# A second copy of x, laid out as features by tokens, in place of the transposes of x on TensorE

## The chip, the core and the metric

The kernel runs on one core of one Trainium2 chip. The metric is the device time of one execution in microseconds (us); lower is better. A core has five engines with a queue of instructions each: TensorE (PE; its weight loads are listed as PEld), VectorE (DVE), ScalarE (ACT), GpSimd (POOL) and SyncE (SP), which here issues nearly all DMA transfers. An engine works through its queue in order and waits on semaphores of the others. SBUF is the working memory of 128 partitions, PSUM the memory into which TensorE writes, in banks of 128 x 512 float32.

## The reference

Of the trunk in the reference only one layer is run (DEPTH is 1): sliding-window attention with a learned sink for each head, and a final norm.

```python
xn = rms_norm(x, norm_g)                       # x: 1 x 4096 x 1024, float32
q, k, v, z = split(xn @ w_in)                  # widths 1024, 256, 256, 1024
o = banded_attention(q, k, v, t5_table, 128, sinks)   # 16 heads of 64, 4 key groups, window 128
x = x + (merge_heads(o) * silu(z)) @ w_out     # w_out: 1024 x 1024
out = rms_norm(x, final_g)
```

rms_norm multiplies a token's row by 1 / sqrt(mean of its squares + 1e-6), the token's factor, and by a vector over the features.

## The kernel before

The 4096 tokens are worked on in 16 blocks of 256 (blocks 0 to 15 here, `tb` in the code, each of two halves `t` of 128 tokens). A product of float32 matrices is made of three products of float16 halves: each factor is split into a high half (rounded to float16, by ScalarE) and a low half (the rest, by VectorE), and high x high, high x low and low x high are summed in PSUM. The weights are loaded once, scaled and split (`load_w`, `split_w`), and the output weights are combined for Strassen's seven products, split and put back into DRAM (`split_wo`), from which each block loads them again (`load_s`).

What a block does with x. `load_x` brings two tiles `xin` of 128 tokens x 1024 features. `x_norm` sums the squares on ScalarE, into a tile `junk` that nobody reads, and gets the factors `rr` by VectorE and GpSimd. `x_scale` multiplies the tile by them, on ScalarE (in block 0 on VectorE); the factor is one number for each partition there, since tokens lie on the partitions. The projections need features on the partitions, so `x_turn` transposes 128x128 squares on TensorE into a PSUM bank `tp`, four for each of four calls, and splits the bank into the halves `xT`. The projections (`proj_t`, `proj_v`) go into banks `pj`; ScalarE and VectorE read them out to `q`, `k`, `v` and `z`. Attention is done by `Pair` objects, four for each block: scores into banks `s` (`scores`), bias and maximum on VectorE (`post`), exponentials on ScalarE (`exps`), sums, scaling and float16 halves `ph` (`halves`), their transposes into `tp` (`turn`), products with v into `o` (`values`) and the gate (`gate`). Then come seven output products (`split_y`, `product`, `add_product`), the residual `res` (loaded by `load_r`), the last norm (`out_norm`) and the store. A buffer is a slot in a rotating pool: the tag "ld" has 5 tiles of 512 KB for `xin`, `res` and the pieces of weights, "tp" has two PSUM banks, "op" four tiles for the halves of the output products.

The order of the work: the text lists every step in a table of slots, 28 for each block, and the steps of a block reach into the next block's slots (a block's x is prepared in the slots of the block before). The builder (`TileContext` with a simulated timeline) may then move an instruction ahead of others on its engine when its inputs are there earlier, so the order on an engine is that of the built program, not of the text. The lines in the text for x are

```python
at(before, s0 + (10 if tb else 4), load_x, tb + 1, t)
at(before, s0 + (12 if tb else 9), x_norm, tb + 1, t)
at(before, s0 + (14 if tb else 10), x_scale, tb + 1, t)
...
at(before, s0 + (18, 19, 25, 27)[j], x_turn, tb + 1, j)
```

Of the kernel before, what the change touches and what calls it, by code (L numbers as in the profile page):

```python
# [18 lines left out]
H = 16  # L19
# [12 lines left out]
# Powers of two that keep both halves of every split inside float16's normal range.  # L32
# [11 lines left out]
def one_hot_buckets():  # L44
    """Row b marks the places y of the circulant row where the distance (127 - y) mod 128 falls in bucket b."""
# [13 lines left out]
def tile_swa_block(ctx, tc, x, t5, norm_g, final_g, w_in, sinks, w_out, hot, out):  # L59
# [12 lines left out]
    # ---------------------------------------------------------------- loads that start at once  # L72
    gs = const.tile([P, KC], F32, name="gs")
    junk = const.tile([P, D], F16, name="junk")
    mhalf = const.tile([P, 1], F32, name="mhalf")
    nc.vector.memset(mhalf, -0.5)
    # The table of functions is loaded while the first inputs are on their way.
    nc.scalar.activation(junk[:, 0:1], mhalf, AF.Square)
    xin = {}

    def load_x(tb, t):
        xin[tb, t] = work.tile([P, D], F32, tag="ld", name="xin", bufs=5)
        r0 = tb * TB + t * P
        nc.sync.dma_start(xin[tb, t], x[r0:r0 + P, :])

# [8 lines left out]
    def load_w(n, j):  # L94
        tag, bufs = (("ld", 5), ("ws", 4))[j % 2]
        st = work.tile([P, 2, 512], F32, tag=tag, name="wst", bufs=bufs)
        src = w_in[2 * j * P:(2 * j + 2) * P, GROUPS[n]:GROUPS[n] + 512]
        nc.sync.dma_start(st, src.rearrange("(c p) f -> p c f", p=P))
        return st

    def split_w(n, j, st):
        for a in range(2):
            kc = 2 * j + a
            g1 = gs[:, kc:kc + 1]
            if n[0] == "z":
                # Heads (2 gp, r) and (2 gp + 1, r) share a block of 128 rows of the output.
# [11 lines left out]
    # Strassen's seven products for blocks of tokens by halves of the features: each one's factors, as signed blocks  # L118
    # (row, column), and the signed blocks of the result to which it goes.
# [11 lines left out]
    def combine(blocks, of):  # L131
        """The signed sum of one or two blocks."""
# [8 lines left out]
    def load_wo(c):  # L141
        st = []
        for gp in range(2):
            w = work.tile([P, D], F32, tag="ld", name="wst", bufs=5)
# [13 lines left out]
    # ---------------------------------------------------------------- constants  # L158
# [15 lines left out]
    # Masks the keys before the sequence's start, for the first block of queries alone.  # L174
# [7 lines left out]
    # ---------------------------------------------------------------- stages of a token block  # L182
    xs = {}

    def x_norm(tb, t):
        rs = work.tile([P, 1], F32, tag="rs", name="rs", bufs=2)
        nc.scalar.activation(junk, xin[tb, t], AF.Square, accum_out=rs)
# [6 lines left out]
    def x_scale(tb, t):  # L194
        if tb:
            nc.scalar.activation(xin[tb, t], xin[tb, t], AF.Copy, scale=xs[tb, t])
        else:
            nc.vector.tensor_scalar(xin[tb, t], xin[tb, t], xs[tb, t], None, op0=OP.mult)
# [3 lines left out]
    def x_turn(tb, j):  # L202
        """Two of the eight blocks of 128 features, transposed and split."""
        p = ps("tp", 2)
        pv = p.rearrange("p (c t) -> p c t", c=2)
        for a in range(2):
            for t in range(2):
                kc = 2 * j + a
                nc.tensor.transpose(pv[:, a, t * P:(t + 1) * P], xin[tb, t][:, kc * P:(kc + 1) * P], ident)
        d = work.tile([P, 2, 2, TB], F16, tag="xT", name="xT", bufs=6)  # L210
        nc.scalar.activation(d[:, :, 0, :], pv, AF.Copy)
        nc.vector.tensor_tensor(d[:, :, 1, :], pv, d[:, :, 0, :], op=OP.subtract)  # L212
# [10 lines left out]
    def proj_t(tb, n, c, p, a):  # L223
        """Features by tokens: block c of the weights n, into half a of a bank."""
# [9 lines left out]
    def evac_q(tb, gp, b, p):  # L234
        """Bank b of half gp: heads 4 b to 4 b + 3 of the half; float16 halves one above the other."""
# [44 lines left out]
    def evac_z(tb, gp, b, p):  # L280
        """2 PROJ silu(z) = (tanh(z / 2) + 1) PROJ z"""
# [345 lines left out]
```

## Time and profile before

| | |
|---|---|
| median of 3 runs | 1498.71 us (1497.95 to 1503.4) |
| the profiled execution: span from its first to its last instruction | 1502.1 us |
| TensorE busy | 1444.3 us, 96%, 12086 matmuls |
| VectorE busy | 1160.7 us, 77%, 3410 instructions |
| ScalarE busy | 740.7 us, 49%, 2036 instructions |
| GpSimd busy | 276.0 us, 18%, 251 instructions |
| DMA | 194.21 MB, 129 GB/s on average |

The profile page gives no time for its execution beside the span; the span is inside the range of the three runs. Busy time is the time in which an engine has at least one instruction under way. TensorE's matmuls are pipelined: the next begins while the last one's end is on its way, so the listed durations add up to more than the time that they take, and the time between the starts of neighbours says what one costs in a full queue.

### The profile page before, as it was taken

What the parts mean: (1) busy time and instruction counts of PE and PEld (TensorE: products, weight loads), DVE (VectorE), ACT (ScalarE), POOL (GpSimd) and SP (SyncE); (2) the same over time, 40 slices, a digit from 0 to 9 for tenths busy, and PEclk for the clock granted to TensorE, in tenths of its full rate; (3) what the DMA queues carried; (4) which work ended last, traced back from release to release, by engine and by line L of the source; (5) the groups of instructions that cost most, each with busy time, mean ns of one, the idle gap of its engine ahead of it and who ended that gap; (6) DMA issues with size and microseconds to landing.
All of it is one profiled execution on the core that took longest, in us unless ns stands there. A gap on an engine that the chain in (4) does not pass through costs nothing. (4 is left out here: it accounts for less than half of the span.)

```text
span 1502.1 us, 31168 instructions
## 1 busy us (share of the span) xinstructions
PE 1444.3 (96%) x12086; PEld 1089.4 (73%) x12086; DVE 1160.7 (77%) x3410; ACT 740.7 (49%) x2036; POOL 276.0 (18%) x251
## 2 busy tenths in 40 slices
PE   7869999999999999999999999999999999999996
PEld 6757777777768777777777777777777776777862
DVE  8799777778777777777778777787777777777896
ACT  8555454535545445454535545445454444544453
POOL 0241212102121211212102121111212112121123
PEclk9989999999999999999999999999999999999998
DMA  9764343514244242343413234241342523334065
GB/s 305 214 218 130 114 138 113 170 61 141 81 133 149 85 155 76 108 141 113 163 64 129 97 114 168 84 149 59 132 141 91 166 80 104 124 113 155 8 217 168
DMA packets 60501, 194.21 MB, mean 129 GB/s; under 512 B 7456, under 2 KB 9536, under 8 KB 60352
## 3 DMA queue, kind: packets, MB, share of 16 engines
q1 hardware_dynamic: 59312, 192.22, 39.1%
q8 instruction: 94, 1.54, 0.4%
q14 instruction: 55, 0.45, 0.1%
q10 hardware_dynamic: 1040, 0.00, 0.0%
HBM read 167.03 MB, written 25.17 MB: 128 GB/s over the span
## 5 line engine op out<-in xcount | busy, mean ns | idle before, releaser
L228 PE MATMUL pj<-xT,wh_q 128*128 128x256 f16 x2048 | 357.2, 275 | 0.8 <-DVE xT L212 0.5
L228 PE MATMUL pj<-xT,wh_z 128*128 128x256 f16 x2048 | 348.9, 273 | 0.1
L373 ACT ACTIVATE c<-c,nm 128x128 f32<-128x128 f32 x512 | 199.0, 389 | 254.0 <-DVE nm L367 254.0
L456 PE MATMUL pj<-ws,yo 128*128 128x512 f16 x1344 | 313.8, 381 | 2.5 <-DMA ws<-wos 1.6
L228 PE MATMUL pj<-xT,wl_q 128*128 128x256 f16 x1024 | 281.0, 275 | 0.0
L228 PE MATMUL pj<-xT,wl_z 128*128 128x256 f16 x1024 | 279.9, 273 | 0.0
L456 PEld LDWEIGHTS <-yo 128*128 128x128 f16 x1344 | 127.9, 98 | 142.6 <-issue 11.4
L228 PEld LDWEIGHTS <-wh_q 128*128 128x128 f16 x2048 | 199.3, 99 | 33.2 <-issue 11.3
L228 PEld LDWEIGHTS <-wh_z 128*128 128x128 f16 x2048 | 196.7, 98 | 36.5 <-issue 12.8
L470 POOL TENSOR_TENSOR res<-res,mc 128x512 f32<-128x512 f32 x80 | 102.3, 1278 | 516.6 <-ACT mc L465 383.9
L138 POOL TENSOR_TENSOR sum<-y 128x512 f32<-128x512 f32 x80 | 106.7, 1342 | 456.8 <-DVE y L427 284.5
L349 DVE COPY_PREDICATED s<-sel,s 128x128 f32<-128x128 int32 x256 | 72.7, 289 | 110.7 <-PE s L339 108.7
L387 ACT ACTIVATE ph<-c 128x512 f16<-128x512 f32 x128 | 80.2, 626 | 105.1 <-DVE c L385 100.8
L339 PE MATMUL s<-k,q 128*128 128x192 f16 x1024 | 126.6, 247 | 4.3 <-DVE c L356 4.2
L358 DVE CUSTOM_DVE_ANT_0 c<-s,bias 128x128 f32<-128x128 f32 x496 | 122.6, 284 | 2.8
L398 PE MATMUL tp<-ident,ph 128*128 128x128 f16 x1024 | 92.4, 221 | 29.6 <-ACT ph L387 19.3
L242 ACT ACTIVATE q<-pj 64x512 f16<-64x512 f32 x128 | 75.4, 589 | 83.8 <-PE pj L228 81.2
L401 DVE TENSOR_TENSOR po<-tp,own_m 128x1024 f16<-128x1024 f16 x128 | 87.9, 686 | 34.9 <-PE tp L398 34.3
L398 PEld LDWEIGHTS <-ph 128*128 128x128 f16 x1024 | 68.2, 98 | 62.3 <-ACT ph L387 32.9
L228 PEld LDWEIGHTS <-wl_z 128*128 128x128 f16 x1024 | 100.4, 98 | 17.1 <-issue 5.8
L228 PEld LDWEIGHTS <-wl_q 128*128 128x128 f16 x1024 | 100.9, 99 | 12.3 <-issue 0.5
L381 DVE TENSOR_TENSOR ls<-l,es 128x4 f32<-128x4 f32 x128 | 60.2, 471 | 62.8 <-ACT es L376 61.1
(89 smaller groups left out, 2358.4 us busy)
## 6 DMA issues: line engine op xcount, KB each, us to landing
ws<-wos SPq DMA_DIRECT2D x224, 512.0 KB, 4.7
xin<-in_x SPq DMA_DIRECT2D x32, 512.0 KB, 6.2
res<-in_x SPq DMA_DIRECT2D x32, 512.0 KB, 5.1
out<-res SPq DMA_DIRECT2D x32, 512.0 KB, 5.7
wst<-in_a_w_in SPq DMA_DIRECT2D x20, 512.0 KB, 9.2
wos<-wo SPq DMA_DIRECT2D x28, 256.0 KB, 2.8
wst<-in_a_w_out SPq DMA_DIRECT2D x16, 256.0 KB, 4.0
scr<-row SPq DMA_DIRECT2D x1, 1024.0 KB, 15.8
```

The costliest lines, as they stand in the source:

```text
L138: nc.gpsimd.tensor_tensor(s, of(a, b), of(c, d), op=OP.add if sign > 0 else OP.subtract)
L228: nc.tensor.matmul(p[:, a * TB:(a + 1) * TB], wx(n, wi, kc, c), xx(tb, xi, kc), start=k == 0, stop=k == 23)
L242: nc.scalar.activation(dst, pv[e * HD:(e + 1) * HD], AF.Copy, scale=SQ / PROJ)
L339: nc.tensor.matmul(s[:, hp, 0:3 * HD], lhs, rhs, start=hl == 0, stop=hl == 1)
L349: nc.vector.copy_predicated(dst, sel[:, None, :].to_broadcast([P, 2, HD]), src)
L358: nc.vector.tensor_tensor_reduce(out=cu, in0=sv, in1=b, scale=1.0, scalar=-3e38, op0=OP.add, op1=OP.max, accum_out=self.m[e][:, u:u + 1])
L373: nc.scalar.activation(cu, cu, AF.Exp, bias=nm[:, u:u + 1], scale=1.0 / SCORE, accum_out=self.l[e][:, u:u + 1])
L387: nc.scalar.activation(ph[:, 0], c, AF.Copy, scale=SP)
L398: nc.tensor.transpose(p[:, l, 2 * hp:2 * hp + 2, r * HD:(r + 1) * HD], self.ph[e][:, l, u, :], ident16)
L401: nc.vector.tensor_tensor(self.po[e], p8, own_m[:, None, :].to_broadcast([P, 8, P]), op=OP.mult)
L456: nc.tensor.matmul(p, YO[i][:, yi, c * P:(c + 1) * P], WO[i, c // 2][:, c % 2, wi, :], start=k == 0, stop=k == 11)
L470: nc.gpsimd.tensor_tensor(r, r, m, op=OP.add if sign > 0 else OP.subtract)
```

## The change

The host gives x a second time, `in_xt`: for each block of 256 tokens 128 partitions x 8 blocks of features x 256 tokens. `load_x` brings, besides `xin`, four tiles `xf` of 2 x 128 features by 256 tokens (256 KB each). `xin` is now used for the sums of squares alone. `x_row` turns the factors of the tokens into rows: a column of 128 factors, read as a 128x128 square with equal columns, is transposed on TensorE into a `tp` bank, twice for a block, so that every partition holds the 256 factors. `x_scale` multiplies an `xf` tile by this row in place, on VectorE, four times for a block. `x_split` makes the halves `xT` from `xf`, with the same two instructions as before, whose input lies in SBUF now.

To make room, "ld" has 4 tiles instead of 5, `junk` is a tile of the tag "op" instead of one of its own, and two small tiles of the bias's preparation share other tags. The products, the attention and the output are as before. Line numbers grow: 228 becomes 236, 398 becomes 406, 456 becomes 464.

```diff
     def load_x(tb, t):
-        xin[tb, t] = work.tile([P, D], F32, tag="ld", name="xin", bufs=5)
+        xin[tb, t] = work.tile([P, D], F32, tag="ld", name="xin", bufs=4)
         r0 = tb * TB + t * P
         nc.sync.dma_start(xin[tb, t], x[r0:r0 + P, :])
+        for j in (2 * t, 2 * t + 1):
+            xf[tb, j] = work.tile([P, 2, TB], F32, tag="xf", name="xf", bufs=4)
+            nc.sync.dma_start(xf[tb, j], xt[tb, :, 2 * j:2 * j + 2, :])
...
+    def junk():
+        return work.tile([P, D], F16, tag="op", name="junk", bufs=4)
...
-        nc.scalar.activation(junk, xin[tb, t], AF.Square, accum_out=rs)
+        nc.scalar.activation(junk(), xin[tb, t], AF.Square, accum_out=rs)
...
-    def x_scale(tb, t):
-        if tb:
-            nc.scalar.activation(xin[tb, t], xin[tb, t], AF.Copy, scale=xs[tb, t])
-        else:
-            nc.vector.tensor_scalar(xin[tb, t], xin[tb, t], xs[tb, t], None, op0=OP.mult)
+    rows = {}
+
+    def x_row(tb):
+
+        p = ps("tp", 2)[:, 0:TB]
+        for t in range(2):
+            nc.tensor.transpose(p[:, t * P:(t + 1) * P], xs[tb, t].to_broadcast([P, P]), ident)
+        rows[tb] = p
+
+    def x_scale(tb, j):
+        f = xf[tb, j]
+        nc.vector.tensor_tensor(f, f, rows[tb][:, None, :].to_broadcast([P, 2, TB]), op=OP.mult)
...
-    def x_turn(tb, j):
-        """Two of the eight blocks of 128 features, transposed and split."""
-        p = ps("tp", 2)
-        pv = p.rearrange("p (c t) -> p c t", c=2)
-        for a in range(2):
-            for t in range(2):
-                kc = 2 * j + a
-                nc.tensor.transpose(pv[:, a, t * P:(t + 1) * P], xin[tb, t][:, kc * P:(kc + 1) * P], ident)
+    def x_split(tb, j):
+
         d = work.tile([P, 2, 2, TB], F16, tag="xT", name="xT", bufs=6)
-        nc.scalar.activation(d[:, :, 0, :], pv, AF.Copy)
-        nc.vector.tensor_tensor(d[:, :, 1, :], pv, d[:, :, 0, :], op=OP.subtract)
+        nc.scalar.activation(d[:, :, 0, :], xf[tb, j], AF.Copy)
+        nc.vector.tensor_tensor(d[:, :, 1, :], xf[tb, j], d[:, :, 0, :], op=OP.subtract)
         xT[tb, j] = d
...
-                at(before, s0 + (14 if tb else 10), x_scale, tb + 1, t)
+            at(before, s0 + 16, x_row, tb + 1)
             for j in range(4):
-                at(before, s0 + (18, 19, 25, 27)[j], x_turn, tb + 1, j)
+                at(before, s0 + 17, x_scale, tb + 1, j)
+                at(before, s0 + (18, 19, 25, 27)[j], x_split, tb + 1, j)
...
+    x_row(0)
+    for j in range(4):
+        x_scale(0, j)
```

What this does to the order on the engines, at three places. On TensorE, in the middle of block 4's slots, before: behind the scores (`s`) of a pair come four transposes of x, then a projection (`pj<-xT`); such a group of four stands four times in a block.

```order
L339 LDWEIGHTS q
L339 MATMUL s<-k,q 128x192
L209 MATMUL tp<-ident,xin 128x128 x4
L228 LDWEIGHTS wh_q_79
L228 MATMUL pj<-xT,wh_q_79 128x256
```

And now, a little earlier in the same block: behind the products with v (`o<-pp,v`) stand the two transposes of the factors, then an output product (`pj<-ws,yo`).

```order
L426 LDWEIGHTS v
L426 MATMUL o<-pp,v 64x512
L207 MATMUL tp<-ident,rr 128x128 x2
L464 LDWEIGHTS yo
L464 MATMUL pj<-ws,yo 128x512
```

The four groups are gone from their places and one group of two stands ahead of the output product. The first transposes of the pair's softmax weights (L406) now stand 43 matmuls behind the second group of scores (31 of projections, 12 of an output product), where before (L398) they stood four transposes of x and 24 matmuls behind it.

On VectorE, at the same place of block 4, before: the sum of the exponentials and the scaling of the softmax weights (`ls`, `rl`, `c<-c,rl`), halves of output factors (`yo`), the low half of the softmax weights (`ph`) and the first low half of x (`xT<-tp`).

```order
L381 TENSOR_TENSOR ls<-l,es 128x4
L383 RECIPROCAL rl<-ls 128x4
L466 SCALAR_TENSOR_TENSOR res<-pj,res 128x512
L385 TENSOR_TENSOR c<-c,rl 128x512
L450 TENSOR_TENSOR yo<-sum,yo 128x512 x2
L450 TENSOR_TENSOR yo<-y,yo 128x512
L349 COPY_PREDICATED s<-sel,s 128x2x64
L388 SCALAR_TENSOR_TENSOR ph<-c,ph 128x512
L212 TENSOR_TENSOR xT<-tp,xT 128x2x256
```

And now: the four multiplications (`xf<-xf,tp`) stand ahead of that sum, and two low halves of x (`xT<-xf`) between it and the scaling.

```order
L212 TENSOR_TENSOR xf<-xf,tp 128x512 x4
L357 COPY_PREDICATED s<-sel,s 128x2x64
L389 TENSOR_TENSOR ls<-l,es 128x4
L220 TENSOR_TENSOR xT<-xf,xT 128x2x256
L366 ISA c,m<-s,bias 128x128
L366 ISA m 128x1
L366 ISA c,m<-s,bias 128x128
L366 ISA m 128x1
L391 RECIPROCAL rl<-ls 128x4
L474 SCALAR_TENSOR_TENSOR res<-pj,res 128x512
L458 TENSOR_TENSOR yo<-sum,yo 128x512
L220 TENSOR_TENSOR xT<-xf,xT 128x2x256
```

The sum, the scaling and the halves of this pair have moved behind the four multiplications and two splits.

In SP's queue at the start, before (`wst` are pieces of weights, `scr` and `bias` the table of biases): the bias is issued ahead of the last piece of the input weights.

```order
L98 DMA wst<-in_a_w_in 128x2x512 x5
L84 DMA xin<-in_x 128x1024 x2
L98 DMA wst<-in_a_w_in 128x2x512 x2
L305 DMA scr<-row 1024x1x256
L98 DMA wst<-in_a_w_in 128x2x512 x5
L310 DMA bias<-scr 64x8x192 x2
L98 DMA wst<-in_a_w_in 128x2x512
L147 DMA wst<-in_a_w_out 64x1024 x6
```

And now:

```order
L88 DMA xf<-in_xt 128x512 x3
L102 DMA wst<-in_a_w_in 128x2x512
L88 DMA xf<-in_xt 128x512
L102 DMA wst<-in_a_w_in 128x2x512 x2
L85 DMA xin<-in_x 128x1024
L102 DMA wst<-in_a_w_in 128x2x512 x2
L85 DMA xin<-in_x 128x1024
L102 DMA wst<-in_a_w_in 128x2x512
L313 DMA scr<-row 1024x1x256
L102 DMA wst<-in_a_w_in 128x2x512 x5
L318 DMA bias<-scr 64x8x192 x2
L151 DMA wst<-in_a_w_out 64x1024 x8
```

The transposed x of block 1 has come between the weights (that of block 0 stands ahead of all of them), and the bias has moved behind the last piece.

## Rows read from the trace of the kernel before

**Rows 1.** The page: busy time of each engine with its share of the span and its number of instructions, then the busy share of TensorE and VectorE in 40 equal slices, in tenths.

```profile
PE 1444.3 (96%) x12086; PEld 1089.4 (73%) x12086; DVE 1160.7 (77%) x3410; ACT 740.7 (49%) x2036; POOL 276.0 (18%) x251
PE   7869999999999999999999999999999999999996
DVE  8799777778777777777778777787777777777896
```

**Rows 2.** Busy time in three stretches: start and end, length, then for PE, PEld, DVE, ACT and POOL the busy time and the number of instructions, the granted clock of TensorE (1.00 is 2.4 GHz), the share of the DMA engines and GB/s.

```profile
155.00:1400.00 1245.00, 1228.77 (x10400) 932.21 (x10400) 945.26 (x2840) 601.19 (x1694) 212.19 (x192) 1.00 0.35 117
0.00:155.00 155.00, 126.91 (x1047) 102.17 (x1048) 131.85 (x342) 95.69 (x208) 36.29 (x36) 0.94 0.71 216
1400.00:1502.00 102.00, 88.61 (x644) 54.98 (x640) 83.54 (x229) 43.80 (x136) 27.56 (x23) 0.96 0.44 145
```

**Rows 3.** All waits of TensorE's matmuls in the stretch from 155 to 1400 us: who waited for whom, us in total, times, the longest.

```profile
PE tp L398 <- ACT ph L387: 11.3, 16, 1.3
PE tp L398 <- DVE ph L388: 2.6, 8, 0.5
```

**Rows 4.** Groups of TensorE's instructions in the same stretch: the transposes of x, their count, busy time and mean ns of one.

```profile
L209 PE MATMUL tp<-ident,xin 128*128 128x128 f32 x224 | 33.6, 273 | 0.0
```

**Rows 5.** Timeline of TensorE around a group of four transposes: start, time until the last one's end, line, tiles, count.

```profile
521.55 0.49 PE L339 MATMUL s<-k,q 128*128 128x192 f16 x4
...
521.88 0.60 PE L209 MATMUL tp<-ident,xin 128*128 128x128 f32 x4
...
522.32 0.38 PE L228 MATMUL pj<-xT,wh_q 128*128 128x256 f16 x2
```

**Rows 6.** Groups of the whole span by shape, for VectorE and ScalarE: busy time and mean ns of one, then the idle time ahead of them and what ended it.

```profile
L385 DVE TENSOR_TENSOR c<-c,rl 128x512 f32<-128x512 f32 x128 | 96.9, 757 | 2.5
...
L387 ACT ACTIVATE ph<-c 128x512 f16<-128x512 f32 x128 | 80.2, 626 | 105.1 <-DVE c L385 100.8 <-DVE mx L365 3.2
L466 DVE SCALAR_TENSOR_TENSOR res<-pj,res 128x512 f32<-128x512 f32 x112 | 75.9, 679 | 6.1 <-ACT mc L465 5.0
...
L450 DVE TENSOR_TENSOR yo<-sum,yo 128x512 f16<-128x512 f32 x80 | 54.8, 698 | 2.1 <-ACT yo L449 2.1
...
L212 DVE TENSOR_TENSOR xT<-tp,xT 128x512 f16<-128x512 f32 x64 | 43.5, 681 | 0.4 <-ACT xT L211 0.4
...
L211 ACT ACTIVATE xT<-tp 128x512 f16<-128x512 f32 x64 | 37.6, 588 | 4.5 <-PE tp L209 4.2
L450 DVE TENSOR_TENSOR yo<-y,yo 128x512 f16<-128x512 f32 x32 | 35.7, 1117 | 0.0
L196 ACT ACTIVATE xin<-xin,rr 128x1024 f32<-128x1024 f32 x30 | 34.0, 1135 | 0.0
```

**Rows 7.** The time around 525 us, in block 5's slots: the busy times from 519.65 to 532.57 us (columns as in rows 2), then pieces of the timelines of VectorE and GpSimd.

```profile
519.65:532.57 12.92, 12.92 (x114) 10.62 (x113) 12.64 (x33) 8.24 (x23) 5.40 (x4) 1.00 0.43 142
...
523.80 1.75 DVE L450 TENSOR_TENSOR yo<-y,yo 128x512 f16<-128x512 f32 x1
...
534.48 0.69 DVE L286 SCALAR_TENSOR_TENSOR z<-z,pj 128x512 f32<-128x512 f32 x1
535.09 0.68 DVE L401 TENSOR_TENSOR po<-tp,own_m 128x1024 f16<-128x1024 f16 x1
535.69 0.68 DVE L404 TENSOR_TENSOR pp<-tp,prev_m 128x1024 f16<-128x1024 f16 x1
...
523.36 1.65 POOL L138 TENSOR_TENSOR sum<-y 128x512 f32<-128x512 f32 x1 [1.23 <-DVE yo L450]
```

**Rows 8.** Timeline of TensorE: the first transposes of x for block 3 and for block 15.

```profile
250.60 0.60 PE L209 MATMUL tp<-ident,xin 128*128 128x128 f32 x4
...
1338.74 0.60 PE L209 MATMUL tp<-ident,xin 128*128 128x128 f32 x4
```

**Rows 9.** A row of all waits of the span: ScalarE's sum of squares waits for the load of x (columns as in rows 3).

```profile
ACT junk L187 <- DMA xin<-in_x: 90.0, 28, 7.4
```

**Rows 10.** Busy times in stretches of the first 100 us (columns as in rows 2).

```profile
0.00:20.00 20.00, 9.90 (x49) 7.38 (x50) 13.83 (x36) 15.34 (x26) 1.85 (x9) 1.00 0.94 326
20.00:40.00 20.00, 20.00 (x182) 17.37 (x180) 17.54 (x39) 16.51 (x26) 1.47 (x2) 1.00 0.98 292
...
60.00:80.00 20.00, 16.64 (x140) 13.74 (x138) 19.78 (x52) 12.05 (x35) 8.49 (x7) 0.92 0.56 175
80.00:100.00 20.00, 15.02 (x119) 11.65 (x116) 19.77 (x49) 10.02 (x24) 10.03 (x7) 0.83 0.67 212
...
60.00:65.00 5.00, 4.84 (x31) 3.53 (x30) 4.95 (x14) 3.02 (x6) 2.65 (x3) 0.68 0.67 217
...
80.00:85.00 5.00, 2.27 (x15) 1.61 (x13) 4.93 (x18) 2.88 (x6) 1.26 (x1) 0.53 0.55 179
```

**Rows 11.** The end of the weights' loading: from the timelines the issue of the last piece on SP's queue and who gets going with it on ScalarE, VectorE and TensorE (in brackets the idle time ahead of it and what ended it), and from the list of DMA issues the two transfers of the bias, KB each and median us to landing.

```profile
42.85 0.38 SPq L98 DMA_DIRECT2D wst<-in_a_w_in  x1
...
55.28 1.33 ACT L110 ACTIVATE wh_z<-wst,gs 128x512 f16<-128x512 f32 x2 [5.28 <-DMA wst<-in_a_w_in]
...
56.03 1.67 DVE L112 SCALAR_TENSOR_TENSOR wl_z<-wst,gs,wh_z 128x256 f16<-128x256 f32 x4 [4.97 <-ACT wh_z L110]
...
59.09 0.50 PE L339 MATMUL s<-k,q 128*128 128x192 f16 x4 [4.08 <-DVE c L356]
...
bias<-scr SPq DMA_DIRECT2D x2, 384.0 KB, 13.0
```

More of the change, by code (lines that the diff above doesn't have):

```diff
@@ L58, in tile_swa_block @@
 @with_exitstack
-def tile_swa_block(ctx, tc, x, t5, norm_g, final_g, w_in, sinks, w_out, hot, out):
+def tile_swa_block(ctx, tc, x, xt, t5, norm_g, final_g, w_in, sinks, w_out, hot, out):
     nc = tc.nc
@@ L73, in tile_swa_block @@
     gs = const.tile([P, KC], F32, name="gs")
[L74 removed]
     mhalf = const.tile([P, 1], F32, name="mhalf")
     nc.vector.memset(mhalf, -0.5)
[L78 to L79 removed]
+    warm = const.tile([P, 1], F32, name="warm")
+    nc.scalar.activation(warm, mhalf, AF.Square)
+    xin, xf = {}, {}
     def load_x(tb, t):
[L82 removed]
+        xin[tb, t] = work.tile([P, D], F32, tag="ld", name="xin", bufs=4)
         r0 = tb * TB + t * P
         nc.sync.dma_start(xin[tb, t], x[r0:r0 + P, :])
+        for j in (2 * t, 2 * t + 1):
+            xf[tb, j] = work.tile([P, 2, TB], F32, tag="xf", name="xf", bufs=4)
+            nc.sync.dma_start(xf[tb, j], xt[tb, :, 2 * j:2 * j + 2, :])
     load_x(0, 0)
@@ L94, in load_w @@
     def load_w(n, j):
-        tag, bufs = (("ld", 5), ("ws", 4))[j % 2]
+        tag, bufs = (("ld", 4), ("ws", 4))[j % 2]
         st = work.tile([P, 2, 512], F32, tag=tag, name="wst", bufs=bufs)
@@ L143, in load_wo @@
         for gp in range(2):
-            w = work.tile([P, D], F32, tag="ld", name="wst", bufs=5)
+            w = work.tile([P, D], F32, tag="ld", name="wst", bufs=4)
             for g in range(2):
@@ L295, in make_bias @@
         nc.sync.dma_start(th, t5)
-        hb = const.tile([BUCKETS, 2 * WIN], F32, name="hb")
+        hb = work.tile([BUCKETS, 2 * WIN], F32, tag="mc", name="hb", bufs=2)
         nc.sync.dma_start(hb, hot)
@@ L301, in make_bias @@
         nc.tensor.matmul(pe[:H, :2 * WIN], th, hb, start=True, stop=True)
-        row = const.tile([H, 2 * WIN], F32, name="row")
+        row = work.tile([H, 2 * WIN], F32, tag="sum", name="row", bufs=2)
         nc.vector.tensor_scalar(row, pe[:H, :2 * WIN], SCORE, None, op0=OP.mult)
@@ L434, in load_r @@
     def load_r(tb, t):
-        R[tb, t] = work.tile([P, D], F32, tag="ld", name="res", bufs=5)
+        R[tb, t] = work.tile([P, D], F32, tag="ld", name="res", bufs=4)
         r0 = tb * TB + t * P
@@ L474, in out_norm @@
         ss = work.tile([P, 1], F32, tag="ss", name="ss", bufs=2)
-        nc.scalar.activation(junk, r, AF.Square, accum_out=ss)
+        nc.scalar.activation(junk(), r, AF.Square, accum_out=ss)
         ms = work.tile([P, 1], F32, tag="oms", name="oms", bufs=2)
@@ L578, in tile_swa_block @@
         x_norm(0, t)
-        x_scale(0, t)
+    x_row(0)
+    for j in range(4):
+        x_scale(0, j)
     staged = [(n, j, load_w(n, j)) for n, j in order[:3]]
     for j in range(4):
-        x_turn(0, j)
+        x_split(0, j)
     for n, j, w in staged:
@@ L615, in give @@
         args.append(nc.dram_tensor(name, a.shape, mybir.dt.from_np(a.dtype), kind="ExternalInput").ap())
+    x = np.asarray(inputs["x"]).reshape(NTB, TB, KC, P)
     shapes = {"x": (T, D), "norm_g": (D,), "a_w_in": (D, -1), "a_sinks": (H,), "a_w_out": (D, D)}
@@ L620 @@
         give(f"in_{n}", a.reshape(shapes[n]) if n in shapes else a)
+        if n == "x":
+            give("in_xt", x.transpose(0, 3, 2, 1))
     give("in_hot", one_hot_buckets())
```

## The prediction

> **What bounds the kernel now.** I read the busy times and the 40 slices of the page first, then the busy time of three stretches. TensorE is busy for 96% of the span, VectorE for 77%, ScalarE for 49% [rows 1]. Busy TensorE alone proves little, since matmuls overlap, so the reader should look at the stretches [rows 2]: from 155 to 1400 us TensorE is busy 1228.77 of 1245 us, VectorE 945.26 (76%). Before 155 us it is the other way: TensorE 126.91 of 155, VectorE 131.85, DMA 71%. After 1400 us VectorE has 83.54 of 102.
>
> Then the waits of TensorE in the long stretch [rows 3]: 11.3 + 2.6 = 13.9 us, all of them the transposes of the softmax weights waiting for the float16 halves. That is 1.1% of 1245 us. So in this stretch, which holds fourteen of the sixteen token blocks, TensorE's own instructions set the time, and what is taken off TensorE should come off the span. In the first 155 us that doesn't hold: there the weights' transfers and VectorE decide.
>
> **What the change takes from TensorE.** The long stretch has 224 transposes of x, 16 for each of 14 blocks, listed with 273 ns each [rows 4]. That duration is not the price: instructions overlap. The timeline shows the price [rows 5]: four transposes start at 521.88, the next matmul at 522.32, so four take 0.44 us and one 0.11 us. 224 x 0.11 = 24.6 us go. The change adds two transposes for each block (the token factors as rows), of the same shape: 28 x 0.11 = 3.1 us come. Net: **-21.5 us**. If the two new ones cost their full 0.273 us each, it would be 28 x 0.163 = 4.6 us less gain; if they hid in a wait, 3.1 more.
>
> The Trainium skill ("TensorE: Matmul & The Clock Gate", Part 4: PE-mode transpose) says that a transpose takes about 275 ns within a kernel and that access latency dominates it. The row's 273 ns agrees as a duration, the starts 0.11 us apart don't as a price; by the page the net gain would be some 14 x 14 x 0.275 = 54 us, an estimate from its figure. That is a rival below.
>
> **What it adds to VectorE, and takes from ScalarE.** Each block gets four multiplications of 128x512 float32, one operand in PSUM. The trace has no such instruction; the nearest are the addition of a product to the residual, 679 ns (one operand in PSUM, in place), and the broadcast scaling of the softmax weights, 757 ns [rows 6]. Starts of neighbours are 0.6 us apart [rows 7]. I take 0.6 us, between 0.58 and 0.76: 4 x 0.6 = 2.4 us per block. ScalarE loses two scalings of 1135 ns for each block and copies from SBUF instead of PSUM (626 against 588 ns) [rows 6]; at 49% busy this is worth nothing directly, at best shorter waits for the halves.
>
> The low halves of x were computed from PSUM (681 ns); now both operands lie in SBUF. The trace has such an operation in two states [rows 6]: 698 ns for the sums, but 1117 ns for the single blocks, and one at 523.80 us that took 1.75 us while GpSimd's addition ran from 523.36 us for 1.65 us [rows 7]. So one of the four per block, or two, may take 0.4 to 1.1 us longer. The Trainium skill ("SBUF — State Buffer", Who interferes with whom) has the rule: a VectorE instruction with two SBUF inputs contends with a GpSimd instruction that reads SBUF, and the later one waits for the whole of the other; with at most one such input it doesn't. The rows agree: 1117 ns with two, 679 with one in PSUM. By the rule the new splits pay and the new multiplications don't; without it both would cost some 0.6 us.
>
> So VectorE gets 2.4 us and up to 2.2 us of stretching on top of some 69 us for a block of 90.7 us (blocks 3 to 15 start their transposes from 250.60 to 1338.74 us, twelve steps: 1088.1 / 12 = 90.7 us) [rows 8]. On average that fits. Locally it doesn't: the four multiplications stand one behind the other just ahead of the softmax sums, and from 519.65 to 532.57 VectorE is busy 12.64 of 12.92 us [rows 7]. What stands behind them is late by 2.4 us and more: the sums, the scaling and the halves of the same pair. The order of TensorE now has the transposes of these halves some 3 us later, with projections and an output product ahead of them, and VectorE has slack behind this window. I cost the added waits at 0.2 us a block, **+3 us**; below, all 13.9 us of waits vanish; above, the burst passes straight to TensorE, 14 x 2.4 = 33.6 us.
>
> **The queue of SP.** Each block gets 1 MB more: at a mean DMA share of 0.35 in the long stretch [rows 2] it fits. The four new transfers stand in SP's queue ahead of the weights of later products and wait there for the buffer that the split releases; the x load itself is waited for by ScalarE even now (90.0 us over 28 times) without TensorE waiting for it [rows 9, 3]. Cost nothing; if the cover goes, a product waits some 2 us, which is part of the fourth case below.
>
> **The first 155 us.** Here two things are paid. First, transfers: 2 MB of transposed x join the weights, at some 300 GB/s 7 us [rows 10]. Now the last weight piece is issued at 42.85 us behind the bias and ScalarE gets it at 55.28; VectorE waits 4.97 us for that and TensorE 4.08 us at 59.09 [rows 11]. The new order issues the bias (13.0 us to landing) behind all weights. Then the bias is late instead of the last piece. Between 0, if the better order pays for everything, and 7: I take 3 us. Second, VectorE: from 60 to 100 us it is 99% busy [rows 10], and block 1 adds 2.4 us there (its scaling was ScalarE's), 4.4 with stretched splits. I take 2.4. The first matmul starts later too, by some 2 us: the second half of x arrives behind 512 KB of transposed x, 1.6 us at 326 GB/s, and row and multiplication take the place of cold transposes; but TensorE idles at 55 us anyway and this goes into that wait. Together **+5.4 us**, between 0 and 12. A change of the granted clock, which is 0.53 to 0.68 in slices behind such waits [rows 10], is inside these bounds.
>
> The last 100 us have no work on x: nothing.
>
> **Sum.** -21.5 + 3 + 5.4 = -13.1 us. The profiled execution (span 1502.1 us, the only time the page has for it) lies 3.4 us above the median of 1498.71 us and inside the three runs. The difference goes onto either: a span of 1489, and **1485.6 us** as median. 0.5%, 7.5 us, is about what a measurement can tell, so faster means under 1491.2 and slower over 1506.2 us.
>
> **Rivals.**
> 1. The gain arrives whole: the head costs nothing, since the wait at 55 us absorbs it and the bias no longer delays the last weights, and ScalarE's relief shortens TensorE's waits. -21.5 - 0 to 13.9: 1463 to 1477 us. For it: TensorE waits only for halves, and ScalarE's part of these is 11.3 of 13.9 us. Against: the halves come after the burst on VectorE.
> 2. The head takes more: 7 us of transfers and 4.4 of VectorE, and waits of 0.2 to 0.5 us a block: -21.5 + 11.4 + 3 to 7 = -7 to -3: 1492 to 1496 us, no change that can be told.
> 3. The burst becomes the wait, the slower side: in every block the softmax chain behind the four multiplications reaches TensorE late by their whole 2.4 us. -21.5 + 33.6 + 5.4 = +17.5: 1516 us. It decides from the point where a block waits more than 21.5 - 5.4 = 16.1 us / 14 = 1.15 us longer, and slower by 0.5% needs 1.7 us. For it: the full window in rows 7, and that all TensorE waits hang on this chain. Against: in that window TensorE doesn't wait at all now, and other work stands ahead of the late transposes.
> 4. A transpose is worth its listed duration, 0.273 us: 196 x 0.273 = 53.5 us, less 8.4: 1454 us. Against: the starts in rows 5.
>
> **Chances.** The forecast, 1477 to 1492 us: 0.56. Rival 1: 0.14. Rival 2, reaching to 1503: 0.16. Rival 3: 0.12. Rival 4: 0.02. The range of 8 in 10 leaves out rival 3, rival 4 and the lower part of rival 1: 1473 to 1503 us. Faster: 0.54 + 0.14 + 0.02, less a little for the forecast's upper edge, 0.67; within 0.5%: 0.20; slower: 0.13.
>
> **What the profile would show.** Right: blocks 3 to 15 start their row transposes 89.4 us apart (90.7 - 1.5 + 0.2); the row transposes' neighbours start 0.22 us later; the multiplications last 0.6 to 0.7 us and the splits 0.7 to 1.1; TensorE's wait at the end of the weights is 3 us later or longer. Wrong: steps of 92 us with TensorE waiting for the halves behind the burst (rival 3); steps of 87 us (rival 4); a head 12 us late (rival 2), or one that isn't late (rival 1).

## The result, and the profile after

The changed kernel takes 1458.64 us (median of 4 runs, 1457.2 to 1460.27), the kernel before 1499.03 beside it: a ratio of 0.9724, 95% interval 0.9711 to 0.9737. That is faster by 40 us, three times the 13.1 us forecast, and 14 us below the range.

The page of the changed kernel, its busy times and slices [rows 1]:

```profile
PE 1404.9 (96%) x11862; PEld 1065.0 (73%) x11862; DVE 1166.2 (80%) x3472; ACT 706.7 (49%) x2006; POOL 281.7 (19%) x251
PE   5888899999999999999999999999999999999995
DVE  7899887878878787887868788787887878778994
```

The stretches [rows 2], columns as there, the last one shorter since the span ends at 1456.3 us:

```profile
0.00:155.00 155.00, 124.46 (x1055) 98.10 (x1055) 135.77 (x357) 91.15 (x207) 37.35 (x36) 0.98 0.78 243
155.00:1400.00 1245.00, 1240.48 (x10575) 946.39 (x10573) 996.26 (x3033) 596.60 (x1749) 229.74 (x202) 1.00 0.40 133
1400.00:1456.30 56.30, 39.97 (x235) 20.46 (x234) 34.22 (x86) 18.98 (x51) 14.62 (x13) 0.88 0.41 140
```

TensorE went from 1228.77 to 1240.48 busy us of 1245, with 224 fewer transposes of x to do. The waits of its matmuls for the halves of the softmax weights [rows 3] are nearly gone; all waits in the same stretch now:

```profile
PE s L347 <- DVE m L366: 2.2, 1, 2.2
PE tp L406 <- ACT ph L395: 1.5, 1, 1.5
PE tp L406 <- DVE ph L396: 0.4, 1, 0.4
PE pj L464 <- DMA ws<-wos: 0.2, 1, 0.2
```

The timeline of TensorE at the row transposes of blocks 3, 4, 5 and 15 [rows 8]:

```profile
243.87 0.43 PE L207 MATMUL tp<-ident,rr 128*128 128x128 f32 x2
...
330.47 0.43 PE L207 MATMUL tp<-ident,rr 128*128 128x128 f32 x2
...
417.07 0.43 PE L207 MATMUL tp<-ident,rr 128*128 128x128 f32 x2
...
1283.07 0.43 PE L207 MATMUL tp<-ident,rr 128*128 128x128 f32 x2
```

The steps are 86.60 us, each the same to 0.01, where they were 90.7 and uneven: next to nothing is waited for any more. By the first scores of the blocks, the gain up to block 2 is 0.85 us (236.86 to 236.01 us), from block 2 to 14 it is 48.94 us (1088.14 to 1039.20), and from there to the end 3.93 us are lost (177.12 to 181.05). Together that is 45.9 us, the difference of the two profiled spans (1502.1 and 1456.3); the medians are 40.4 us apart, so what is counted per block from these two executions may be up to 0.4 us too large. So the question is the 4.1 us per block: the transposes were costed at 14 x 0.11 = 1.5 of them.

**Where the row misled.** The same stretch of the kernel before has waits in a second row, that of the weight loads, which stand ahead of the matmuls. Before, and then after:

```profile
PEld L398 <- ACT ph L387: 21.1, 31, 1.6
...
PEld L398 <- DVE ph L388: 11.7, 36, 0.6
```

```profile
PEld L406 <- ACT ph L395: 1.7, 1, 1.7
PEld L406 <- DVE ph L396: 1.5, 2, 0.9
```

These are 32.8 us over 67 waits, where the matmuls' rows had 13.9 us over 24. A matmul's idle time is counted from the listed end of the one before, 0.27 us behind its start where the next could start after 0.11, so a part of each wait lies under a modelled end. The Trainium skill ("Perfetto Trace Analysis", Tensor Engine Instruction (MATMUL, LD_WEIGHTS)) says that a TensorE duration in a trace is a model and no measurement; these rows agree. By starts alone, each gap against the usual spacing of its kind, I count 2.1 us per block ahead of these transposes before, some 28 us in all, and none after.

**Whom they waited for.** Counted from a block's first transposes of x, the gaps stand at 10 to 12 us (the block's first pair) and at 45 to 57 us (the third). ScalarE before, at a third pair:

```profile
464.89 1.05 ACT L475 ACTIVATE junk<-res 128x1024 f16<-128x1024 f32 x1
465.84 0.19 ACT L475 ACTIVATION_READ_ACCUMULATOR junk<-res 128x1 f32 x1
471.08 1.06 ACT L187 ACTIVATE junk<-xin 128x1024 f16<-128x1024 f32 x1 [5.05 <-DMA xin<-in_x]
...
472.53 0.40 ACT L373 ACTIVATE c<-c,nm 128x128 f32<-128x128 f32 x1 [0.30 <-DVE nm L367]
```

And VectorE there, with the sums of squares (`ms`) ahead of the pair's `nm`:

```profile
472.26 0.15 DVE L189 TENSOR_SCALAR ms<-rs 128x1 f32<-128x1 f32 x1 [1.45 <-ACT junk L187]
472.33 0.16 DVE L367 TENSOR_SCALAR nm<-mx 128x4 f32<-128x4 f32 x1
```

ScalarE stands 5 us at x_norm's Square for x's transfer, and the pair's exponentials wait behind it. I had dismissed this wait [rows 9] as costing TensorE nothing. In the changed kernel the Square stands behind a pair's halves, an evacuation of q, the exponentials and two yo, and waits for nothing:

```profile
464.81 0.61 ACT L457 ACTIVATE yo<-y 128x512 f16<-128x512 f32 x1
465.32 1.04 ACT L194 ACTIVATE junk<-xin 128x1024 f16<-128x1024 f32 x1
```

Three theories: **A**, ScalarE's standing (or its load) at the third pair; **B**, the place of the softmax-weight transposes in TensorE's order, later in the changed kernel; **C**, rival 4, no real waits and a dear transpose: it had named steps of 87 us.

### The profile page after: what moved, and what is told of

It reads as the page before. It is cut to its first block, busy times and chain, and to the rows that moved or that the text cites. A ratio compares the mean times of both kernels' runs of the same rounds, so it can differ in the third digit from the quotient of the medians.

```text
span 1456.3 us, 30910 instructions
## 1 busy us (share of the span) xinstructions
PE 1404.9 (96%) x11862; PEld 1065.0 (73%) x11862; DVE 1166.2 (80%) x3472; ACT 706.7 (49%) x2006; POOL 281.7 (19%) x251
## 4 chain that ended last, share of the span: by engine, by line
PE 84%; DVE 9%; DMA 3%; ACT 2%; issue 1%; POOL 0%; SPq 0%; POOLq 0%; DVEq 0%; ACTq 0%
PE pj L236 46%; PE pj L464 18%; PE o L426 6%; PE pj L277 5%; PE s L347 5%; PE tp L406 3%; DMA wst<-in_a_w_in 2%; ACT c L381 1%; DVE wo L159 1%; DVE c L366 1%; DVE c L393 1%; DMA wst<-in_a_w_out 1%; DVE ph L396 1%; DMA ws<-wos 1%; DVE q L254 1%
## 5 line engine op out<-in xcount | busy, mean ns | idle before, releaser
L236 PE MATMUL pj<-xT,wh_q 128*128 128x256 f16 x2048 | 349.9, 274 | 8.0 <-ACT xT L219 4.4
L236 PEld LDWEIGHTS <-wh_z 128*128 128x128 f16 x2048 | 196.8, 98 | 33.3 <-issue 10.5
L347 PE MATMUL s<-k,q 128*128 128x192 f16 x1024 | 130.6, 246 | 8.6 <-DVE c L364 4.3
L250 ACT ACTIVATE q<-pj 64x512 f16<-64x512 f32 x128 | 75.5, 590 | 122.7 <-PE pj L236 120.1
L347 PEld LDWEIGHTS <-q 128*128 128x128 f16 x1024 | 90.7, 98 | 26.4 <-DVE m L366 5.3
L393 DVE TENSOR_TENSOR c<-c,rl 128x512 f32<-128x512 f32 x128 | 106.9, 835 | 3.0
L254 DVE SCALAR_TENSOR_TENSOR q<-pj,q 64x256 f16<-64x256 f32 x256 | 98.2, 419 | 10.8 <-ACT q L250 6.8
## 6 DMA issues: line engine op xcount, KB each, us to landing
xf<-in_xt SPq DMA_DIRECT2D x64, 256.0 KB, 3.1
wos<-wo SPq DMA_DIRECT2D x28, 256.0 KB, 3.5
wst<-in_a_w_out SPq DMA_DIRECT2D x16, 256.0 KB, 7.4
```

The lines of the kernel that those rows point to most:

```text
L236: nc.tensor.matmul(p[:, a * TB:(a + 1) * TB], wx(n, wi, kc, c), xx(tb, xi, kc), start=k == 0, stop=k == 23)
L254: nc.vector.scalar_tensor_tensor(q[HD:, :, h, :], pv[e * HD:(e + 1) * HD, c], SQ / PROJ, q[0:HD, :, h, :], op0=OP.mult, op1=OP.subtract)
L347: nc.tensor.matmul(s[:, hp, 0:3 * HD], lhs, rhs, start=hl == 0, stop=hl == 1)
L393: nc.vector.tensor_tensor(c, c, rl[:, :, None].to_broadcast([P, 4, P]), op=OP.mult)
```

## The experiments

Ratios are to the kernel before in the same series, which took 1499.3 to 1501.0 us. The changed kernel was timed beside the kernel before at 1499.03 us alone, so what is said against it below is said across series, and differences of 3 us aren't told apart with certainty. "Step" is the mean distance of the first softmax-weight transposes of blocks 3 to 13 in the trace (90.7 before, 86.60 after). "Standing" is ScalarE's wait for xin from 155 to 1400 us (84.8 before, not listed after).

**1. The scaling alone on VectorE.** In `x_scale`:

```diff
-        if tb:
+        if tb < 0:
```

> The kernel before with one step moved: the scaling of x in blocks 1 to 15 runs on VectorE (two operations of 128x1024 per block, as block 0 always had it) and no longer on ScalarE (there two of 1.135 us). Transposes, order of the slots and loads are as before. Theory A (the waits of 2.1 us per block that vanished were late softmax weights, late because ScalarE carried x's scaling and stood for x's transfer): ScalarE gains 2.3 us per block, VectorE loses about 1.5, so a part of the waits ahead of the softmax-weight transposes goes; 1480 to 1495 us, steps between blocks of 89.3 to 90.5 (90.7 before). Theory B (the waits vanished because the program places these transposes later on TensorE): no change, 1495 to 1505, or a little slower by VectorE. Theory C (there was hardly a wait; a transpose of x costs TensorE its listed 0.273 us): no change, 1499.

1499.44 us, 1.0004 (0.9985 to 1.0022); step 90.1 in the profiled execution, which was the fastest of ten (1497.17 us), standing 94.9. Taking the load from ScalarE is worth nothing that the time shows: if A holds, it is the standing.

**2. x's load six slots earlier.**

```diff
-at(before, s0 + (10 if tb else 4), load_x, tb + 1, t)
+at(before, s0 + (4 if tb else 4), load_x, tb + 1, t)
```

> The kernel before with x's load for the next block called in slot 4 of a block in place of slot 10, so that ScalarE's x_norm no longer stands for the transfer (5 us of standing per block before). Theory A: that standing, with VectorE blocked behind it, is the larger part of what makes the softmax weights of the second pair late; the waits there (about 1.6 us per block) go wholly or mostly: 1477 to 1490 us, steps of 89.1 to 90. Theory B: no change, 1495 to 1503. Theory C: no change.

1487.51 us, 0.9910 (0.9881 to 0.9939); step 89.6, standing 47.1; the gaps fall to 1.0 us per block. As A has it, and against B and C.

**3. The softmax-weight transposes one slot later** (the values and the gate with them; `w` is `s + 1` up to block 14):

```diff
-at(first, s + 5, pr.turn, 0)
+at(first, w + 5, pr.turn, 0)
```

> The kernel before with the softmax-weight transposes, the values and the gate called one slot (about 3 us of TensorE's work) later in blocks 0 to 14; nothing else. Theories A and B both say that the wait ahead of these transposes is real and is bridged by other work: it goes, some 1.5 to 2.1 us per block, 1468 to 1480 us, steps of 88.5 to 89.2. Theory C: the waits are only 0.3 us per block, 1494 to 1500, steps over 90.3.

1473.73 us, 0.9824 (0.9790 to 0.9858); step 88.7. The waits of the first pair are gone but for 0.16 us per block, 1.2 us at the third stay, standing 83.2. So B is a part, not all. C falls.

**4. 16 transposes per block put back into the changed kernel**, in `x_split`:

```diff
+        if tb:
+            p = ps("tp", 2)
+            for a in range(2):
+                for t in range(2):
+                    nc.tensor.transpose(p[:, (2 * a + t) * P:(2 * a + t + 1) * P],
+                                        xf[tb, j][:, a, t * P:(t + 1) * P], ident)
```

> The changed kernel with 16 float32 transposes per block put back (240 in all, of the second copy of x, in the four slots where the splits of x are), whose results nobody reads; ScalarE's and VectorE's work is as in the changed kernel. Theories A and B: each costs TensorE 0.11 us and the waits do not come back, 1458.6 + 26 = 1485 us (1482 to 1489), steps of 88.4. If the waits come back with the transposes, 1505 to 1515. Theory C: 240 x 0.273 = +65, 1524 us, steps of 91.

1485.80 us, 0.9901 (0.9873 to 0.9929); 27 us more than the changed kernel, 0.11 us for each of 240. By starts the 16 take 1.75 us per block, as before the change (1.74). One wait of 0.7 us per block came with them; the first blocks made up for it (the third's softmax-weight transposes begin at 252.2 us, 256.0 in the changed kernel). So the time agrees with the starts in part by luck, and the price rests on the starts. C is dead, and rival 4 with it: its 1454 us and its steps of 87 us were nearly those measured, by luck, for another reason.

**5. and 6. Buffers of its own for x** (two, and three left in ld), alone and with the later slot:

```diff
-xin[tb, t] = work.tile([P, D], F32, tag="ld", name="xin", bufs=5)
+xin[tb, t] = work.tile([P, D], F32, tag="xi", name="xin", bufs=2)
```

> The kernel before with x's tiles in two buffers of their own (tag xi) and three left in the shared tag ld for residuals and staged weights (five together, as before); calls stay in their slots. x's load then waits for no store of a result any more. Theory A: ScalarE's standing of 5 to 7 us at x_norm goes, and with it the waits of TensorE 45 to 57 us into a block, 1.0 to 1.6 us per block: 1475 to 1488 us, up to 5 us worse if the first block's weights now wait for one of three buffers. Theory B: no change, 1495 to 1505.

> The kernel before with both: x's tiles in two buffers of their own, and softmax-weight transposes, values and gate one slot later in blocks 0 to 14. x is still transposed on TensorE and scaled on ScalarE. If A and B each hold their own part of the 2.1 us of waits per block (A the 1.2 us that the later slot alone left at 48 to 50 us into a block, B the rest, and 0.65 us per block of switches around the values that the later slot saved as well), all waits go: steps of 88.0, 1499 - 13.5 x 2.75 = 1462 us (1458 to 1467), as fast as the changed kernel to within 5 us with all the transposes of x still there. If the waits at 48 to 50 us come from something else: 1470 to 1476, as the later slot alone.

1493.19 us, 0.9950 (0.9937 to 0.9964), and 1473.86 us, 0.9823 (0.9801 to 0.9846). Misses: the standing only fell to 63.7 and 57.6, since two tiles that are held until a block's last transposes can't be loaded earlier (in the trace of the first, the last four start at 461.24 us and the next load is issued at 461.85). They don't tell A apart.

**7. The changed kernel without its multiplications** in blocks 1 to 15 (the line with `x_scale` dropped):

> The changed kernel without the four multiplications of x by the row factors in blocks 1 to 15: that scaling is left out, while the row factors are still made and turned. VectorE loses 4 x 0.6 to 0.7 us per block. Theory B (the later place of the softmax-weight transposes comes from the burst of multiplications, which the builder of the order foresees): the order goes back to the earlier place and 0.5 us or more of waits per block returns, 1462 to 1470 us. If the later place comes from the rest of the change: no waits, steps of 86.6, 1454 to 1459.

1465.95 us, 0.9776 (0.9754 to 0.9798): less work, and 7 us slower than the changed kernel. Step 87.36. The weight loads in the long stretch:

```profile
PEld L406 <- ACT ph L395: 7.5, 13, 0.6
...
PEld L406 <- DVE ph L396: 4.2, 14, 0.3
```

From the pair's last scores to the transposes of its second half there are 11.6 us here, 14.1 in the changed kernel and 12.1 before; the halves are ready after 12 to 13.5 us in all three. With the multiplications in the program the builder puts other work of TensorE ahead of these transposes; without them they come too early. That is B, for 0.7 us per block. The splits' wait for the row of factors went together with the multiplications, so which of the two the builder's order answers isn't shown.

**8. The later slot in the changed kernel** (edit as in 3):

> The changed kernel with the softmax-weight transposes, values and gate one slot later in blocks 0 to 14. There are no waits left to bridge; what it may save is switches between the forms of the matmuls around the values, 0.8 us per block now and 0.37 where the kernel before got the same shift: steps of 86.2, 1452 us (1448 to 1456). If the later gate makes the products late instead: 1459 to 1465.

1455.32 us, 0.9701 (0.9682 to 0.9721), with run 15 the fastest, some 3 us below the changed kernel, though the intervals of the two ratios overlap. The step is 86.7, not 86.2: the switches around the values fell (the longer distance of starts where one form of matmul follows another, 0.31 us from a product with v to a projection, 0.11 between projections), and 0.9 us per block of new waits came at the first pair. What is gained lies in the last step (71.2 against 75.5 us).

**9. and 10. Four tiles in ld**, as in the changed kernel, alone and with the later slot:

```diff
-xin[tb, t] = work.tile([P, D], F32, tag="ld", name="xin", bufs=5)
+xin[tb, t] = work.tile([P, D], F32, tag="ld", name="xin", bufs=4)
```

> The kernel before with four buffers in place of five in the shared tag ld (x's tiles, residuals, staged weights), which the changed kernel also has; nothing else. In the builder's order the first Square of x_norm then stands on ScalarE behind the four exponentials, two evacuations of q and the splits of the weights that follow it before, so it should no longer stand for x's transfer ahead of them. Theory A, as it now reads (the late softmax weights of 45 to 57 us into a block come from the place of x_norm's Square in ScalarE's order, where ScalarE stands some 5 us for x's transfer with VectorE blocked behind it, and not from ScalarE's load): 1.2 to 1.6 us per block go, 1478 to 1486 us, steps of 89.1 to 89.6, ScalarE's standing for xin under 2 us per block. Theory B alone: no change, 1496 to 1503. Weights staged through four buffers may cost the first block up to 4 us.

> The kernel before with four buffers in ld and with softmax-weight transposes, values and gate one slot later in blocks 0 to 14. All 240 x 16 transposes of x's tiles stay on TensorE and the scaling stays on ScalarE. If A (place of the Square) and B (place of the softmax-weight transposes) are the two halves of the waits, both go, with 0.65 us per block of switches around the values: steps of 88.0 to 88.2, 1458 to 1466 us. If the waits of 48 to 50 us into a block have another cause: 1470 to 1476, as the later slot alone.

(The count of transposes meant there is 16 x 15 = 240.) 1552.17 us, 1.0358 (1.0341 to 1.0375), and 1510.24 us, 1.0090 (1.0061 to 1.0119): slower, against the forecast. ScalarE of the first, at a third pair:

```profile
487.38 1.06 ACT L187 ACTIVATE junk<-xin 128x1024 f16<-128x1024 f32 x1 [3.46 <-DMA xin<-in_x]
488.35 0.19 ACT L187 ACTIVATION_READ_ACCUMULATOR junk<-xin 128x1 f32 x1
488.44 0.61 ACT L387 ACTIVATE ph<-c 128x512 f16<-128x512 f32 x1
```

The Square has moved, as the order said, but x's load has become later too: it waits for the stores of the results (146.8 us in SP's queue, 83.0 before). ScalarE stands as long as ever (80.0), now directly ahead of the halves that TensorE wants, and the gaps rise to 4.5 us per block. So it is not the Square's place as such; the standing is what costs, and most where something urgent is next.

**11. The old scaling kept beside the new in the changed kernel** (two Copies of 1.135 us per block on ScalarE):

> The changed kernel with ScalarE's old work put back beside the new: in blocks 1 to 15 ScalarE still multiplies x's two tiles by their factors (two operations of about 1.135 us per block, results unread). Theory A as it now reads (place, not load): the waits do not come back, steps of 86.6, 1457 to 1461 us. If ScalarE's load of 2.3 us per block was the cause: 0.4 to 1.2 us per block comes back, 1464 to 1475.

1457.87 us, 0.9723 (0.9708 to 0.9737), step 86.60. ScalarE's load is out as a cause from this side too.

**12. Five tiles in ld in the changed kernel**, three for xf:

> The changed kernel with five buffers in ld as before (and three in place of four for the second copy of x, for room). In the builder's order x_norm's Squares stay behind the exponentials and evacuations of q. Theory A (it is the place of the Square that counts): no waits, 1457 to 1461 us. If the number of buffers itself sets the waits: 1470 to 1480. A dearer first block by the third buffer's missing fourth: up to 3 us.

1470.52 us, 0.9805 (0.9791 to 0.9820); step 87.5. A miss. ScalarE doesn't stand here either, yet 1.0 us of gaps per block is back, all at the first pair, whose transposes the builder has placed earlier. That is B again, but two sizes changed, and which of them moved the order wasn't tried.

**13. and 14. The scratch tile alone.** Square writes an elementwise result that nobody reads. Before it went to one constant tile, in the changed kernel it takes one of the tiles op, in turn with the halves yo (the last norm's Square likewise, not shown here):

```diff
+    def junk():
+        return work.tile([P, D], F16, tag="op", name="junk", bufs=4)
...
-        nc.scalar.activation(junk, xin[tb, t], AF.Square, accum_out=rs)
+        nc.scalar.activation(junk(), xin[tb, t], AF.Square, accum_out=rs)
```

> The kernel before with one part of the change that computes nothing: the scratch tile into which Square throws its elementwise result is no longer one constant tile but comes from the four rotating tiles op of the split weights' activations (yo), as in the changed kernel. In the builder's order both Squares of x_norm then stand behind the exponentials, the evacuation of q and the splits yo, just as in the changed kernel; buffers, loads, transposes and scaling are as before. Theory A (ScalarE standing for x's transfer at x_norm makes the softmax weights of 45 to 57 us into a block late): ScalarE's standing for xin falls from 85 us in the long stretch to under 30, and 1.2 to 1.6 us of waits per block go: 1478 to 1486 us, steps of 89.1 to 89.6. If those waits have another cause (the scaling of x on ScalarE, the third transfer): 1495 to 1503.

> The same with softmax-weight transposes, values and gate one slot later in blocks 0 to 14. If the standing (A) and the place of these transposes (B) are the whole of the waits, they all go, with 0.65 us per block of switches around the values: steps of 88.0 to 88.3, 1458 to 1466 us, with every transpose of x still on TensorE and its scaling on ScalarE. If something else holds the weights back at 48 to 50 us: 1470 to 1476.

1481.63 us, 0.9874 (0.9850 to 0.9899), step 88.60 and constant to 0.01; with the later slot 1464.02 us, 0.9751 (0.9728 to 0.9774), step 87.5. ScalarE in the first, the standing that is left in the long stretch, and the weight loads' waits (67 of them, 32.8 us, before):

```profile
468.16 0.61 ACT L452 ACTIVATE yo<-y 128x512 f16<-128x512 f32 x1
468.68 1.04 ACT L190 ACTIVATE junk<-xin 128x1024 f16<-128x1024 f32 x1
```

```profile
ACT junk L190 <- DMA xin<-in_x: 0.5, 1, 0.5
```

```profile
PEld L401 <- ACT ph L390: 4.6, 13, 0.4
PEld L401 <- DVE ph L391: 4.2, 14, 0.3
```

With its buffer in the rotation, the Square comes behind the yo that use the same four tiles, and by then x is there, as in the changed kernel. The gaps at the third pair are gone, the 0.5 us at the first pair stay. TensorE's order doesn't explain it: between the third pair's last scores and the transposes of its two halves there are 21 and 95 other matmuls, where there were 21 and 110, so these transposes don't stand later; but the halves are ready 3.1 and 4.9 us earlier, counted from these scores (medians over ten blocks). A is shown: 19 us for a tile that holds nothing. With both edits, and every transpose and scaling of x still in place, the kernel is within 6 us of the changed one.

**15. The constant scratch tile in the changed kernel:**

> The changed kernel with one constant scratch tile for Square, as before the change. In the builder's order the Squares of x_norm move ahead of the exponentials again (behind one evacuation of q). If the scratch tile is the whole of A: ScalarE stands for xin again, 0.5 to 1.5 us of waits per block come back, 1464 to 1478 us. If x's load, which in the changed kernel waits for no transposes of the block before, has landed by then: no standing, steps of 86.6, 1457 to 1461 us.

1456.30 us, 0.9699 (0.9679 to 0.9720), step 86.6. The Squares move ahead again and ScalarE stands for 48.8 us. TensorE doesn't notice: the halves of the third pair are ready 0.2 to 0.6 us before their transposes, where they had 1.6 to 2.2 us to spare. So between the blocks of the changed kernel the scratch tile isn't needed. The standing is shorter there (48.8 us against 84.8) and the transposes stand later (40 matmuls behind the third pair's last scores, 21 before); that these cover it, and which of them, is argued and not shown.

**16. Values and gate alone one slot later in the changed kernel:**

> The changed kernel with values and gate alone one slot later in blocks 0 to 14, the softmax-weight transposes where they are. Switches around the values fall from 0.8 to about 0.4 us per block without new waits: steps of 86.2, 1452 us (1448 to 1456). If other waits take their place, as with the transposes moved too: 1454 to 1459.

1459.82 us, 0.9721 (0.9700 to 0.9743), step 86.9. No gain: 1.2 us per block of new waits stand against the switches.

## Why the prediction was wrong, step by step

*The transposes, -21.5 us: right.* 16 took 1.74 us per block by starts, two take 0.25; over 14 blocks 20.9 us. Experiment 4 gives the same price by starts. The listed 273 ns would have given 65 us there.

*The waits, +3 us (0.2 per block), with 13.9 us as the most that could go: this step failed, in size and in sign.* The gaps were 2.1 us per block, and all went, together with another 0.5 per block of switches and short waits around the values. Of the 4.1 us per block, 2.1 are what the scratch tile does when it is the only change (90.7 to 88.60), 1.5 are the transposes and 0.5 the first pair's waits, which the later place covers (88.60 to 86.60). In the changed kernel these 2.1 us don't hang on the scratch tile alone: without it, too, the step is 86.6 (experiment 15). Two readings were wrong: the size, from the matmuls' rows alone; and rows 9, where I took "TensorE doesn't wait for it" as "it costs nothing" without following what stood behind ScalarE's Square. I had noted the scratch tile's move in the diff and costed it not at all.

*The burst on VectorE: there, and covered.* The multiplications last 679 ns, as the nearest row said. From the last scores to the last half of the weights the two chains of the first pair grew from 11.95 and 12.76 us to 13.19 and 13.46 (medians over ten blocks). But the transposes now come 13.7 and 14.1 us behind, where it was 10.5 and 12.1. Rival 3 fails as its own "against" said: other work stands ahead of them. Experiment 7 shows that this order comes with the multiplications.

*The stretched splits, up to 2.2 us per block: not seen.* The groups by shape in the changed kernel:

```profile
L393 DVE TENSOR_TENSOR c<-c,rl 128x512 f32<-128x512 f32 x128 | 106.9, 835 | 3.0
...
L220 DVE TENSOR_TENSOR xT<-xf,xT 128x512 f16<-128x512 f32 x64 | 42.2, 682 | 0.5 <-ACT xT L219 0.5
L212 DVE TENSOR_TENSOR xf<-xf,tp 128x512 f32<-128x512 f32 x64 | 39.7, 679 | 1.2 <-PE tp L207 1.2
L458 DVE TENSOR_TENSOR yo<-y,yo 128x512 f16<-128x512 f32 x32 | 22.0, 688 | 0.0
```

*The first 155 us, +5.4 us: too dear.* The first scores of block 0 are 1.95 us later, as forecast, but by those of block 1 the changed kernel is 2.5 us ahead (145.08 against 147.60), some 1.8 of it that block's transposes. Block 2's are only 0.85 us ahead, and a wait of 2.2 us for VectorE follows at 162 us. The 4 us at the end of the weights' loading are gone. Two blocks' transposes would be 3.0 us, so by these marks the head lies between a gain of 1 us and a cost of 2. Part of that is the scratch tile's: without it (experiment 15) the first scores of block 2 come at 239.85 us in place of 236.01, and in the kernel before it alone moved them from 236.86 to 233.22; with the later slot they moved the other way (236.82 to 238.31). These are single executions, and TensorE's granted clock up to 155 us also rose, from 0.94 to 0.98; what each is worth in the head wasn't tried.

*The end, 0: wrong by 3.9 us,* and again by the scratch tile that was costed at nothing. With that tile as the only difference, the time from the first scores of block 14 to the end grows from 177.12 to 182.94 us (experiment 13), from 168.64 to 175.54 (14 against 3) and from 175.12 to 181.05 (the changed kernel against 15). There the weight loads of the last output products wait for their halves yo, whose tiles Square's scratch now shares. Before, and then after:

```profile
PEld L456 <- DVE yo L450: 1.2, 2, 0.8
PEld L456 <- ACT yo L449: 0.8, 2, 0.4
```

```profile
PEld L464 <- ACT yo L457: 6.0, 3, 3.3
...
PEld L464 <- DVE yo L458: 2.8, 2, 1.8
```

In the changed kernel with a constant scratch tile (experiment 15) they are 1.2 us.

*Rival 1 named the mechanism* ("ScalarE's relief shortens TensorE's waits", a head that absorbs its cost), but bounded it with the same 13.9 us, and experiments 1 and 11 show that it is not relief from work but from standing. With 28 us of waits in place of 13.9 it would have reached down to 1449 us and held the result.

## What to carry to other kernels

Count the waits of a pipelined engine by the starts of its instructions, or in its weight loads' row, before you bound what can be won there. An engine that is half idle can still be the cause: look at what stands behind a long wait in its queue, and whether it is wanted soon. And where a builder orders the work, each edit of buffers is an edit of the order, even of a tile that nobody reads: try each part alone.

## What the runs showed that I had not expected

Removing work made the kernel slower (experiment 7) and so did giving it fewer buffers that it seemed not to need (9), both by the order. On VectorE the long instances moved rather than vanished: `yo<-y` fell from 1117 to 688 ns [rows 6], the scaling of the softmax weights rose from 757 to 835, while the new splits with both operands in SBUF stayed at 682. Which GpSimd addition meets which instruction is, as I read it, again a matter of the order; it wasn't tried.
